# Sliding windows by DMA alone: a twelfth staged batch, and packets of 16 and 32 KB on two rings

## The chip, the cores and the metric

The kernel runs on one core of a Trainium2 chip. The metric is the time of one execution on the device in microseconds; the number given is the median of three runs. One more execution is recorded by the hardware profiler, and the views quoted here come from that execution.

## The reference

The input `x` has 32 batches of 4096 rows of 256 float32 values. Windows of 64 rows are taken at every 32nd row, 127 per batch, and each window is copied to its place in the output:

```python
n_windows = (length - window_size) // stride + 1        # 127
result = np.zeros((batch, n_windows, window_size, dim), dtype=np.float32)
for i in range(n_windows):
    start = i * stride
    result[:, i] = x[:, start:start + window_size].copy()
```

There is no arithmetic. A block is 32 rows, 32 KB; a batch is 128 blocks, 4 MB. A window is two neighbouring blocks, 64 KB, so nearly every block is written twice: once as the second half of a window and once as the first half of the next. The output of a batch is 127 windows, about 8 MB.

## The kernel before

The kernel consists of DMAs and waits only; no compute engine works on data. A batch reaches the output in one of two ways.

*Copied batches* (21 of 32) go from DRAM to DRAM. `_Kernel.copy` (L91) issues three DMAs on SP's queue for each: windows 0 to 63 (`WHOLE = 64`), windows 64 to 111, and the last 15. Source rows of 64 KB start 32 KB apart and so overlap; output rows of 64 KB lie behind each other. `start` (L59) takes `parts`, which limits the size of a piece to 64 KB divided by `parts`: the first 64 windows go in pieces of 64 KB, the rest in pieces of 32 KB.

*Staged batches* (11 of 32, the odd numbers 1 to 21 in `STAGED`) go through SBUF, on ACT's queue. `load` (L73) reads a batch into one of five tiles (`BUFS`) of 128 partitions of one 32 KB block each; `store` (L81) writes the tile out twice, as the first halves of the windows and as the second halves. All pieces are 32 KB. Each store covers 128 windows where a batch has 127: the surplus half window falls into the neighbouring batch's output, the first half of the next batch's window 0 or the second half of the previous batch's last window. That is why the staged batches are every other one, and why the neighbours of a staged batch have to be written after its stores.

ACT's loop issues load n+1, waits for load n, and issues the two stores of batch n. From the sixth load on, a load waits for the stores that used its tile five batches earlier.

SP issues the copies in the order that `_order` (L99) gives. The `EARLY` batches (18, 20, 22) come first: they are copied before their staged neighbours are stored, ACT waits for them (`all_of`, L63) before the first store beside them, and their damaged half windows are written again at the end, by small DMAs of one block in 16 pieces of 2 KB (`half`, L44). Then come batches without a staged neighbour. A batch with staged neighbours (a "tied" one) is put in at a position worked out from the last staged neighbour's place `behind`, `ceil((behind + 2) * n / len(STAGED))` with n = 21 copied batches, and before it SP waits for the stores of its neighbours (`after_store`, L69).

At the end SP waits for the stores beside the early batches and for the early copies, issues the small DMAs for the damaged halves, and then waits for everything.

Of the kernel before, what the change touches and what calls it, by code (L numbers as in the profile page):

```python
# [1 line left out]

# [4 lines left out]


STAGED = tuple(range(1, 22, 2))
BUFS = 5  # L10

WHOLE = 64

EARLY = (18, 20, 22)


class _Geometry:


    def __init__(self, x, out, W, S):  # L20
        self.B, self.L, self.D = x.shape
        self.x, self.out = x, out
        self.n_win = (self.L - W) // S + 1
        self.n_blk = self.L // S
        self.blk = S * self.D
        self.win = W * self.D
        assert W == 2 * S and self.n_blk == self.n_win + 1 == 128

    def src(self, b, block, dims):

        at = (b * self.n_blk + block) * self.blk
        return bass.AP(self.x.tensor, self.x.offset + at, dims)

    def dst(self, b, half, dims):

        at = b * self.n_win * self.win + half * self.blk
        return bass.AP(self.out.tensor, self.out.offset + at, dims)

    def rows(self, b, w0, n):

        s, d = [[self.blk, n], [1, self.win]], [[self.win, n], [1, self.win]]
        return self.dst(b, 2 * w0, d), self.src(b, w0, s)

    def half(self, b, half, block):  # L44

        dims = [[self.blk // 16, 16], [1, self.blk // 16]]
        return self.dst(b, half, dims), self.src(b, block, dims)


class _Kernel:  # L50
    def __init__(self, nc, g, tiles):
        self.nc, self.g, self.tiles = nc, g, tiles
        self.loaded = [nc.alloc_semaphore(f"loaded{i}") for i in range(len(tiles))]
        self.stored = [nc.alloc_semaphore(f"stored{i}") for i in range(len(tiles))]
        self.copied = nc.alloc_semaphore("copied")
        self.early = nc.alloc_semaphore("early")
        self.count = {}

    def start(self, engine, out, in_, sem, parts=1):  # L59
        engine.dma_start(out=out, in_=in_, max_dma_last_dim=65536 // parts).then_inc(sem, 16)  # L60
        self.count[id(sem)] = self.count.get(id(sem), 0) + 16

    def all_of(self, engine, sem):  # L63
        engine.wait_ge(sem, self.count[id(sem)])

    def slot(self, n):
        return divmod(n, len(self.tiles))

    def after_store(self, engine, n):  # L69
        turn, i = self.slot(n)  # L70
        engine.wait_ge(self.stored[i], 32 * (turn + 1))

    def load(self, n):  # L73

        g, (_, i) = self.g, self.slot(n)
        if n >= len(self.tiles):
            self.after_store(self.nc.scalar, n - len(self.tiles))
        src = g.src(STAGED[n], 0, [[g.blk, g.n_blk], [1, g.blk]])
        self.start(self.nc.scalar, self.tiles[i][:, :], src, self.loaded[i])

    def store(self, n):  # L81

        g, (turn, i) = self.g, self.slot(n)
        self.nc.scalar.wait_ge(self.loaded[i], 16 * (turn + 1))
        for half in (0, -1):
            dst = g.dst(STAGED[n], half, [[g.win, g.n_blk], [1, g.blk]])
            self.start(self.nc.scalar, dst, self.tiles[i][:, :], self.stored[i])

    def copy(self, b, sem):  # L91

        n, nc = self.g.n_win, self.nc
        self.start(nc.sync, *self.g.rows(b, 0, WHOLE), sem)
        self.start(nc.sync, *self.g.rows(b, WHOLE, n // 16 * 16 - WHOLE), sem, 2)
        self.start(nc.sync, *self.g.rows(b, n // 16 * 16, n % 16), sem, 2)


def _order(B):  # L99


    near = {b for s in STAGED for b in (s - 1, s + 1)}
    order = list(EARLY) + [b for b in range(B) if b not in near and b not in STAGED]
    tied = sorted(near - set(EARLY))
    n = len(order) + len(tied)
    for b in tied:
        behind = max(STAGED.index(s) for s in (b - 1, b + 1) if s in STAGED)
        order.insert(-(-(behind + 2) * n // len(STAGED)), b)
    return order


@with_exitstack
def kernel(
    ctx: ExitStack,
    tc: tile.TileContext,
    x: bass.AP,
    window_size: bass.AP,
    stride: bass.AP,
    out: bass.AP,
):  # L120
    nc = tc.nc
    W, S = int(window_size), int(stride)
    g = _Geometry(x, out, W, S)
    assert 0 not in STAGED and g.B - 1 not in STAGED
    pool = ctx.enter_context(tc.tile_pool(name="blocks", bufs=1))
    tiles = [pool.tile([g.n_blk, g.blk], x.dtype, name=f"xb{i}") for i in range(BUFS)]

    with tc.tile_critical():
        k = _Kernel(nc, g, tiles)
        for b in _order(g.B):  # L130
            if b not in EARLY:
                for s in (b - 1, b + 1):
                    if s in STAGED:
                        k.after_store(nc.sync, STAGED.index(s))
            k.copy(b, k.early if b in EARLY else k.copied)
        k.load(0)
        waited = False
        for n, s in enumerate(STAGED):
            if n + 1 < len(STAGED):
                k.load(n + 1)  # L140
            if not waited and (s - 1 in EARLY or s + 1 in EARLY):
                k.all_of(nc.scalar, k.early)
                waited = True
            k.store(n)


        for n, s in enumerate(STAGED):
            if s - 1 in EARLY or s + 1 in EARLY:
                k.after_store(nc.sync, n)
        k.all_of(nc.sync, k.early)  # L150
        for b in EARLY:
            if b - 1 in STAGED:
                k.start(nc.sync, *g.half(b, 0, 0), k.copied)
            if b + 1 in STAGED:
                k.start(nc.sync, *g.half(b, 2 * g.n_win - 1, g.n_blk - 1), k.copied)
        for n in range(len(STAGED)):
            k.after_store(nc.sync, n)
        k.all_of(nc.sync, k.copied)
        for sem in [*k.loaded, *k.stored, k.copied, k.early]:
            nc.sync.sem_clear(sem)  # L160


# [1 line left out]
_INS = ['x', 'window_size', 'stride']  # L164
_OUTS = [((32, 127, 64, 256), 'float32')]

_NUMBERS = {'window_size': 64, 'stride': 32}


# [26 lines left out]
```

## Time and profile before

| what | value |
|---|---|
| median of 3 runs | 770.55 us (769.2 to 771.77) |
| the profiled execution's own time | 772.19 us |
| span in that profile | 770.4 us |
| DMA packets, bytes | 9890, 313.37 MB |
| HBM read, written | 221.09 MB, 267.22 MB |
| copies issued by SP (64, 48 and 15 windows) | 21 of each |
| loads and stores issued by ACT, 4096 KB each | 11 and 22 |
| small DMAs for damaged halves, 32 KB each | 5 |

The span is what the profiler recorded between the first and the last instruction; the device time is a little longer. Queue q1 is SP's ring and q10 is ACT's. Both rings are served by the same sixteen DMA engines. GB/s in the profile counts each byte that a DMA moves once: a copied byte counts once although it is read from and written to HBM. Because no compute engine works, the parts of the page on engines and the chain of work that ended last are nearly empty (four constants set by POOL), and the reading goes by the DMA lines, the waits of SP's queue and the trace's record of every DMA packet (its queue, size, start and duration).

### The profile page before, as it was taken

How to read it: one execution, taken by the hardware profiler on the slowest of the kernel's cores; microseconds unless marked ns; L12 is line 12 of the kernel's file. 1: busy time of each engine (PE TensorE's matmuls, PEld its weight loads, DVE VectorE, ACT ScalarE, POOL GpSimd, SP SyncE). 2: the span in 40 equal slices, each digit the busy share in tenths (PEclk: the TensorE clock that was granted, in tenths of full speed). 3: DMA queues.
4: the chain of work that ended last, by engine and by line, in shares of the span. 5: the costliest groups of instructions: out<-in, count | busy, mean ns of one | idle time of the engine just before them, and what ended most of it. 6: DMA issues, size and time to landing. Idle time of an engine off the chain costs nothing. (4 is left out here: it accounts for less than half of the span.)

```text
span 770.4 us, 179 instructions
## 1 busy us (share of the span) xinstructions
POOL 0.2 (0%) x4
## 2 busy tenths in 40 slices
POOL 0000000000000000000000000000000000000000
DMA  9999999999999999999999999999999999999994
GB/s 381 396 412 436 393 413 419 447 371 434 400 424 395 441 403 424 403 444 386 430 420 422 405 419 419 403 412 419 417 415 427 417 415 412 444 415 432 391 338 178
DMA packets 9890, 313.37 MB, mean 407 GB/s; under 512 B 1595, under 2 KB 1595, under 8 KB 1675
## 3 DMA queue, kind: packets, MB, share of 16 engines
q1 hardware_dynamic: 5137, 174.95, 55.3%
q10 hardware_dynamic: 4752, 138.41, 43.2%
q14 instruction: 1, 0.01, 0.0%
HBM read 221.09 MB, written 267.22 MB: 634 GB/s over the span
## 5 line engine op out<-in xcount | busy, mean ns | idle before, releaser
L177 POOL MEMSET const-bfloat16-1.0<- 128x1 bf16 x1 | 0.1, 101 | 0.0
L177 POOL MEMSET const-uint8-127<- 128x1 uint8 x1 | 0.1, 101 | 0.0
L177 POOL MEMSET const-float32-0.0<- 128x1 f32 x1 | 0.1, 98 | 0.2 <-issue 0.2
L177 POOL MEMSET const-float32-1.0<- 128x1 f32 x1 | 0.1, 98 | 0.0
## 6 DMA issues: line engine op xcount, KB each, us to landing
out_dram<-xb ACTq DMA_DIRECT2D x22, 4096.0 KB, 94.1
out_dram<-in_x_dram SPq DMA_DIRECT2D x21, 3072.0 KB, 118.5
xb<-in_x_dram ACTq DMA_DIRECT2D x11, 4096.0 KB, 129.6
out_dram<-in_x_dram SPq DMA_DIRECT2D x21, 960.0 KB, 124.8
out_dram<-in_x_dram SPq DMA_DIRECT2D x21, 111.2
out_dram<-in_x_dram SPq DMA_DIRECT2D x5, 32.0 KB, 23.1
```

The source lines that it names most:

```text
L177: nc = _bacc.Bacc("TRN2", target_bir_lowering=False, num_devices=1)
```

## The change

`STAGED` grows by batch 23, so that 12 batches are staged and 20 are copied. Loads and stores go in pieces of 16 KB (`2 * BLOCK_PARTS` is 4). A copied batch is issued as 80 windows in pieces of 16 KB, 32 windows in pieces of 32 KB and 15 windows in pieces of 16 KB (`COPY_PARTS`). `EARLY` gets batch 24, the other neighbour of batch 23. In `_order` a tied batch's position takes `behind + 2.5` instead of `behind + 2`. At the end, the small DMAs for the damaged halves are issued store by store, each as soon as its own store has landed, where before all the stores concerned were awaited first; there are seven of them instead of five.

```diff
-STAGED = tuple(range(1, 22, 2))
+STAGED = tuple(range(1, 24, 2))
 BUFS = 5
-WHOLE = 64
-EARLY = (18, 20, 22)
+EARLY = (18, 20, 22, 24)
+BLOCK_PARTS = 2
+COPY_PARTS = ((80, 4), (32, 2), (15, 4))
...
     def load(self, n):
...
-        self.start(self.nc.scalar, self.tiles[i][:, :], src, self.loaded[i])
+        self.start(self.nc.scalar, self.tiles[i][:, :], src, self.loaded[i], 2 * BLOCK_PARTS)
...
     def store(self, n):
...
-            self.start(self.nc.scalar, dst, self.tiles[i][:, :], self.stored[i])
+            self.start(self.nc.scalar, dst, self.tiles[i][:, :], self.stored[i], 2 * BLOCK_PARTS)
...
     def copy(self, b, sem):
-        n, nc = self.g.n_win, self.nc
-        self.start(nc.sync, *self.g.rows(b, 0, WHOLE), sem)
-        self.start(nc.sync, *self.g.rows(b, WHOLE, n // 16 * 16 - WHOLE), sem, 2)
-        self.start(nc.sync, *self.g.rows(b, n // 16 * 16, n % 16), sem, 2)
+        w = 0
+        for rows, parts in COPY_PARTS:
+            self.start(self.nc.sync, *self.g.rows(b, w, rows), sem, parts)
+            w += rows
+        assert w == self.g.n_win
...
-        order.insert(-(-(behind + 2) * n // len(STAGED)), b)
+        order.insert(-(-(2 * behind + 5) * n // (2 * len(STAGED))), b)
...
+        k.all_of(nc.sync, k.early)
         for n, s in enumerate(STAGED):
             if s - 1 in EARLY or s + 1 in EARLY:
                 k.after_store(nc.sync, n)
-        k.all_of(nc.sync, k.early)
-        for b in EARLY:
-            if b - 1 in STAGED:
-                k.start(nc.sync, *g.half(b, 0, 0), k.copied)
-            if b + 1 in STAGED:
-                k.start(nc.sync, *g.half(b, 2 * g.n_win - 1, g.n_blk - 1), k.copied)
+            if s - 1 in EARLY:
+                k.start(nc.sync, *g.half(s - 1, 2 * g.n_win - 1, g.n_blk - 1), k.copied)
+            if s + 1 in EARLY:
+                k.start(nc.sync, *g.half(s + 1, 0, 0), k.copied)
```

More of the change, by code (lines that the diff above doesn't have):

```diff
@@ L137 @@
         waited = False
+        last = len(STAGED) - 1
         for n, s in enumerate(STAGED):
-            if n + 1 < len(STAGED):
+            if n < last:
                 k.load(n + 1)
```

## The prediction

> **What bounds the kernel now.** I read the page's slices and queues first. In the slices, the reader should see that the DMA engines are busy to the last slice but one, while the rate wanders from 371 to 447 GB/s and falls to 178 only at the end.
>
> ```profile
> DMA  9999999999999999999999999999999999999994
> GB/s 381 396 412 436 393 413 419 447 371 434 400 424 395 441 403 424 403 444 386 430 420 422 405 419 419 403 412 419 417 415 427 417 415 412 444 415 432 391 338 178
> DMA packets 9890, 313.37 MB, mean 407 GB/s; under 512 B 1595, under 2 KB 1595, under 8 KB 1675
> ...
> q1 hardware_dynamic: 5137, 174.95, 55.3%
> q10 hardware_dynamic: 4752, 138.41, 43.2%
> ...
> HBM read 221.09 MB, written 267.22 MB: 634 GB/s over the span
> ```
>
> Queue q1 is SP's ring (the copies), q10 is ACT's (staged loads and stores). Together they fill 98.5% of sixteen engines' time, so no engine can be kept busier and no wait hides much. Less time means fewer bytes, or packets that run faster. The waits agree: SP sits 601.5 us behind stores, yet its packets go on at an even rate in every stretch of the records, so its ring is never empty meanwhile.
>
> ```profile
> SPq L71 <- DMA out_dram<-xb: 601.5, 9, 97.0
> SPq L60 <- DMA out_dram<-xb: 85.8, 1, 85.8
> SPq L64 <- DMA out_dram<-in_x_dram: 26.3, 1, 26.3
> ```
>
> The windows show the end. The last store lands at about 738 us (SP issues its last small copies at 738.6), and from there only copies run, much more slowly.
>
> ```profile
> 380.00:420.00 40.00, 0.00 (x0) 1.00 1.01 425
> 420.00:460.00 40.00, 0.00 (x0) 1.00 1.00 406
> ...
> 700.00:737.00 37.00, 0.00 (x0) 1.00 0.97 406
> 737.00:768.00 31.00, 0.00 (x0) 1.00 0.72 257
> ```
>
> Then I tallied the trace's packet records by size. A 32 KB packet takes 1213 ns at best, and 75% of them are within 2 ns of that; the mean is 1254 (copies) and 1260 (staged). A 64 KB packet takes 2418 at best, reached by only 35%; the mean is 2584. A completion record takes 9 ns, and a packet starts 4 ns before its predecessor ends. So an undisturbed packet costs 37.66 ns per KB plus about 4 ns, and everything above that I call stall.
>
> An engine has this work. Copies of 64, 48 and 15 rows give it 4 packets of 64 KB, 6 of 32 KB and 2 of 32 KB per batch. The 15 rows run on 15 engines (q1's 1067 completion records are 42 x 16 + 21 x 15 + 5 x 16), so the sixteenth has less and does not decide. Copy batch: 4 x 2.414 + 8 x 1.209 = 19.33 us; 21 of them are 405.9. Staged batch: one load and two stores of 8 packets, 24 x 1.209 = 29.02; 11 of them are 319.2. With completions the undisturbed work is **725.6 us**. The records' own time on such an engine is 759.2, so stall is **33.6**; the span's other **11.2** are ends (first packet about 2.8 us in, last landing to span end 1.8, the rest engines that finish unevenly).
>
> Where the stall sits: I cut the trace into 5 us stretches and set stall against the copies' share of the bytes. A copied byte is read from and written to HBM, a staged one only read or only written, so HBM traffic is 1 + share per DMA byte. Stretches with a share above 0.62 (41 of 144, 205 us) lose 7.5%, or 15.4 us; the others lose 2.5%, or 12.7 us; those at 0.47 to 0.52 lose 1.6%, with a median of 0.4%. With copies alone at the end 18 to 23% is lost (about 5 us), and at the start 0.7. High shares come when 64 KB copy packets meet 32 KB staged ones: the rings alternate packet by packet, completions included (4627 records on q1 against 4676 on q10 between about 10 and 730 us), so a packet twice as long takes twice the share, 0.667.
>
> **The change, part by part.** *One more batch staged.* It adds 29.02 and removes 19.33 us of work per engine: +9.7 us, all on the path, since the engines have no idle time to put it in. It saves 4.1 MB of HBM reads.
>
> *Smaller packets.* A 16 KB packet has no row in this trace. Between zero and the 4 ns of the larger sizes I take 4, giving 606.5 ns undisturbed. Copies: 24 x 0.6065 + 4 x 1.209 = 19.39, times 20 = 387.8. Staged: 48 x 0.6065 = 29.11, times 12 = 349.3. With completions this makes **737.6**, 12.0 above before: 9.7 from the batch, 2.3 from packet ends.
>
> *What meets what.* 24 of a copy batch's 28 packets now equal the staged ones, a share of 0.5. Only the 32 rows in 32 KB packets make 0.667: 4 turns x 1.82 = 7.3 us of a batch's 36.5 us, 20%, against 4 x 3.62 = 14.5 of 37.4, 39%, before. High shares held 28% of the steady time (engines drift out of step); scaled by 20/39 that is 14.6%. Steady stall is then 0.146 x 7.5% + 0.854 x 1.6% = 2.5% of some 748 us, 18.4. I take 1.6% because that row has the mix the new kernel has; the ends are 0.4% (its median, were the rest spilt over from neighbouring stretches) and 2.5% (all stretches below 0.62), worth 10.8 and 24.2 us.
>
> *The end.* Per engine, q1 now has 20 x (28 + 3) = 620 records and q10 12 x (48 + 3) = 612; before, 315 and 297. SP's ring starts about 4.4 us later, some 7 small packets. So copies run alone for 15 packets of 0.6 us, 9 us, instead of 31, and lose 1.6 instead of about 5. Start: 0.7 as before. Total stall **20.7**. Uneven finishes come from uneven stalls; with about 40% less stall I take 2.5 off the ends, **8.7** (bounds: 11.2, and 4.6 for the latencies alone).
>
> *Waits and order.* `_order` puts a tied copy half a step later and `EARLY` has one more, so five copies instead of four are issued before SP's first wait. SP's stores come back well ahead: it now issues at 95.8 us the copies that start near 133, a lead of 38; in the new order a store ends every 63 us (750 us over twelve), the first near 84, and a copy batch starts every 37.5 us, so that the batch behind store 0 (the sixth, at 187) has a lead of about 100, behind store 1 (the seventh, at 225) 78, and the later ones 75 to 100. A later issue would cost nothing until the ring ran dry. ACT's wait for `early` stands at store 8, some 530 us in, with the four early copies done by about 150. The last halves go from five to seven (32 more packets of 2 KB at about 84 ns over 16 engines: 0.2 us). The last two wait for the last store, behind which 9 us of copies still run and cover two issues of 0.6 us. If the staged ring ended last they would cost about 3 us (1.2 plus 1.9 from issue to first packet, as at the start).
>
> Sum: 737.6 + 20.7 + 8.7 = **767.0 us** of span against 770.4, 3.4 less. The profiled execution took 772.19, and the runs' median is 770.55; 3.4 off the median gives **767.0**, rounded.
>
> Rules that bear on this. The 7.5% above a share of 0.62 and the 323 to 345 GB/s of copies alone (twice that through HBM, up to 690) say that mixing decides. The Trainium skill (HBM Reference, Specifications) gives about 716 GB/s for one HBM domain; an estimate from that page is that a share of 0.667 could still run at about 430 GB/s, so unmixing would bring almost nothing and the sum would be 737.6 + 33.6 + 11.2 = 782. I go by the row. The Trainium skill (DMA: Bandwidth & Descriptors, Latency and other measured facts) also reports that row pitches of large powers of two slow copies; an engine's 64-row share steps 256 KB in the output before and 320 KB with 80 rows, and were that the cause instead, the sum would lose another 6 us (0.146 x the 5.9% between 7.5 and 1.6, of 748). No run here separates the two yet.
>
> **The rivals.**
> *Deeper gain, 0.18.* Even mixing nearly ends the stall: 0.4% in even stretches saves 7.6 more, **759.4**. For it: many 5 us stretches at a share near 0.5 show none at all. Against: the mean is 1.6%.
> *A draw, 0.20.* Stall in even stretches is 2.0% instead of 1.6% (2.6 us more, span 769.6), or the ends stay at 11.2 (769.5), or both (772.1): the gain from mixing then pays for the twelfth batch and no more.
> *Slower, 0.25.* Stall follows bytes, whatever meets what: today's 32 KB records stand 3.4 and 3.8% above their best, and 3.6% of 737.6 is 26.6, with ends of 11.2 **775.4**. It decides once stall passes 24.1 us, or 3.3% of the work (21.6 if the ends don't shrink). Within it, 0.04 for stall per packet: 44 ns on each of 1136 packets is 50 us, **799**. For it: 32 KB records beside 64 KB ones are hardly slower than elsewhere. Against: 64 KB packets reach their best half as often as 32 KB ones, and stall peaks once per copied batch.
> The forecast itself, 0.37, spans 763 to 769 by its own bounds.
>
> **How the numbers follow.** A difference of 0.3% (2.3 us) is about what a measurement can tell here. The forecast and the deeper gain make faster 0.55; the draw makes same 0.20; slower is 0.25. The range leaves out the deepest gain and the per-packet case: 757 to 778, taking in 759.4 and 775.4 with two microseconds about them.
>
> **What would show it.** Right: 16 KB records at 610 ns for most, mean at most 625; q10 ending about 10 us before q1; slices steadier, near 420 to 430 GB/s with no dips below 400; DMA bytes 317.4 MB. Wrong: a 16 KB mean above 633 (stall by bytes), a best above 615 (a price per packet), q10 ending last, or dips that remain with even packets.

## The result, and the profile after

The changed kernel takes 767.25 us (median of 6 runs, 766.43 to 768.4) where the kernel before takes 770.95 (6 runs beside it). The ratio is 0.9949, with a 95% interval of 0.9936 to 0.9962: faster by half a per cent. The profiled execution took 768.4 us, its span is 766.6.

The page's slices, queues and HBM line after the change, to be laid beside those of before:

```profile
DMA  8999999999999999999999999999999999999996
GB/s 371 425 410 421 405 428 431 408 411 427 423 415 421 431 415 425 432 408 416 427 420 417 431 420 420 423 428 410 414 427 419 422 428 418 417 428 421 420 406 237
DMA packets 19837, 317.70 MB, mean 414 GB/s; under 512 B 1628, under 2 KB 1628, under 8 KB 1740
...
q1 hardware_dynamic: 10044, 166.70, 51.9%
q10 hardware_dynamic: 9792, 151.00, 47.3%
...
HBM read 217.02 MB, written 267.35 MB: 632 GB/s over the span
```

Three things are to be seen. The engines move 4.3 MB more and are about as full as before (99.2% against 98.5%), so most of the gain is in how fast packets run. The dips are gone: from the second slice to the last but one the rate lies between 405 and 432, where before it swung from 371 to 447 up to the last two slices. And the two rings hold nearly equal numbers of records (10044 and 9792).

The windows of the end: the staged ring is done at 754 us, and copies run alone for 10 us instead of 31.

```profile
700.00:737.00 37.00, 0.00 (x0) 1.00 0.98 416
737.00:754.00 17.00, 0.00 (x0) 1.00 0.96 401
754.00:764.00 10.00, 0.00 (x0) 1.00 0.55 198
```

The waits of SP's queue (who waited for what; us in total, times, longest) show a change that the prediction did not have:

```profile
SPq L62 <- DMA out_dram<-xb: 61.2, 2, 40.2
SPq L73 <- DMA out_dram<-xb: 19.2, 3, 9.4
SPq L66 <- DMA out_dram<-in_x_dram: 7.7, 1, 7.7
```

SP waited 714 us for stores and copies before and 88 us now. It spends the difference inside its DMA instructions. The durations of these issues (line L62; min/median/max in ns) have become very long:

```profile
L62 SPq DMA_DIRECT2D out_dram<-in_x_dram x67: 510/8114/29578, 0.9 to 756.2; - x67
L62 ACTq DMA_DIRECT2D out_dram<-xb x24: 378/442/625, 20.9 to 672.9; - x24
L62 ACTq DMA_DIRECT2D xb<-in_x_dram x12: 418/13034/19682, 0.9 to 550.1; - x12
```

Before, the medians were 597 ns on SP and 500 ns for ACT's loads; all of SP's DMA instructions together took 50 us before and take 672 now. A load now has twice the packets per engine, and a copied batch 28 where it had 12. I read this as a queue ahead of the engines that fills up, so that the issuing instruction stands until there is room.

**The sum, measured.** By the same tally of packet records, for one of the fifteen full engines:

| us | before | predicted | after |
|---|---|---|---|
| undisturbed work | 726.0 | 737.6 | 738.8 |
| stall | 33.4 | 20.7 | 19.4 |
| ends | 11.0 | 8.7 | 8.5 |
| span | 770.4 | 767.0 | 766.6 |

The tally here takes the undisturbed 16 KB record at its measured 611 ns, and means without the early rounding; that is why before differs by 0.2 to 0.4 from the prediction's figures. Of the 14.0 us less stall, some 10 are steady stall (28.1 and 18.1 us between 5 and 725 us) and most of the rest is the stretch of copies alone at the end.

### The profile page after: what moved, and what is told of

Read it like the earlier page. It is cut to its first block, busy times and chain, and to the rows that moved or that the text cites. A ratio compares the mean times of both kernels' runs of the same rounds, so it can differ in the third digit from the quotient of the medians.

```text
span 766.6 us, 180 instructions
## 1 busy us (share of the span) xinstructions
POOL 0.2 (0%) x4
## 3 DMA queue, kind: packets, MB, share of 16 engines
q1 hardware_dynamic: 10044, 166.70, 51.9%
q10 hardware_dynamic: 9792, 151.00, 47.3%
```

## The experiments

Two theories stood against each other. **Mixing**: stall goes by the copies' share of the bytes that run at a time, since a copied byte passes HBM twice. **Size**: small packets stall less, whatever runs beside them. Two more were to be excluded: that the twelfth batch's saved HBM reads, or the windows' steps in memory, make the gain. All results in one table; "share" and "steady stall" are the means over the 5 us stretches between about 5 and 725 us, "swing" the standard deviation of the share, ratio that to the kernel before, run beside it, with its 95% interval. Work and ends are tallied as above; what the span has beyond the two is stall. Each tally is of the one profiled execution, which lies up to about 1.5 us from its kernel's median, so one or two microseconds between rows say little. How many stretches lie above some share also depends on where the stretches begin (28 to 44 of 144 lie above 0.62 in before); what they lose moves less (7.0 to 7.9%).

| kernel | median us | ratio | span | work | ends | share | swing | steady stall |
|---|---|---|---|---|---|---|---|---|
| before | 770.95 | 1 | 770.4 | 726.0 | 11.0 | 0.548 | 0.098 | 3.9% |
| changed | 767.25 | 0.9949 (0.9936 to 0.9962) | 766.6 | 738.8 | 8.5 | 0.521 | 0.057 | 2.5% |
| uneven | 793.2 | 1.0276 (1.0250 to 1.0302) | 792.5 | 737.6 | 12.3 | 0.563 | 0.200 | 5.75% |
| double | 770.27 | 0.9987 (0.9974 to 0.9999) | 768.0 | 736.0 | 8.6 | 0.513 | 0.074 | 2.6% |
| half | 771.69 | 0.9995 (0.9983 to 1.0008) | 770.1 | 742.4 | 10.7 | 0.525 | 0.054 | 2.2% |
| double_level | 769.32 | 0.9970 (0.9958 to 0.9983) | 768.7 | 735.9 | 10.6 | 0.527 | 0.072 | 3.0% |
| b12_large | 777.88 | 1.0083 (1.0062 to 1.0104) | 775.0 | 735.8 | 10.2 | 0.546 | 0.095 | 3.9% |
| b11_small | 766.28 | 0.9934 (0.9914 to 0.9954) | 765.3 | 728.5 | 8.9 | 0.555 | 0.068 | 3.6% |
| before_tail | 775.42 | 1.0045 (1.0029 to 1.0062) | 773.7 | 725.9 | 10.5 | 0.564 | 0.109 | 5.0% |
| pow2 | 769.35 | 0.9971 (0.9958 to 0.9984) | 767.4 | 738.9 | 8.9 | 0.513 | 0.059 | 2.2% |
| b13 | 772.2 | 1.0004 (0.9990 to 1.0019) | 770.5 | 749.1 | 7.0 | 0.490 | 0.040 | 2.0% |
| b12_even | 767.77 | 0.9953 (0.9939 to 0.9966) | 766.2 | 738.7 | 10.5 | 0.528 | 0.053 | 2.3% |
| b11_even | 768.45 | 0.9963 (0.9951 to 0.9976) | 768.2 | 728.4 | 12.0 | 0.565 | 0.043 | 3.8% |
| b10_even | 767.22 | 0.9946 (0.9927 to 0.9965) | 765.3 | 718.3 | 10.9 | 0.593 | 0.036 | 4.9% |

All edits are to the changed kernel.

### Mixing or size: uneven, double, half

```diff
 # uneven
-COPY_PARTS = ((80, 4), (32, 2), (15, 4))
+COPY_PARTS = ((80, 2), (32, 2), (15, 2))
```

> The changed kernel with all copy packets at 32 KB (380 records per engine on the copies' ring against 612 on the staged one), so that 32 KB copy packets meet 16 KB staged ones and copies hold a share of 0.667 wherever both rings have work; staged packets go alone for the rest. Undisturbed work 737.0 us per engine, 1.2 below the changed kernel's. Mixing theory (stall goes by the copies' share): 7.5 to 8% of the 617 us of shared work, 46 to 49 us of stall, and with ends of 8 a span of 785 to 795. Size theory (small packets stall less, whatever meets what): stall of 20 to 24 us, span 765 to 769.

Span 792.5 with 42.7 us of stall: the mixing theory's 785 to 795, and far from the size theory's 769. Bytes and HBM reads are those of the changed kernel and work is 1.2 us less; only the sizes that meet are others. The page's slices lie below the changed kernel's nearly everywhere, mostly between 385 and 420:

```profile
GB/s 366 396 392 411 393 394 402 403 401 414 422 411 385 417 418 405 393 429 403 423 429 409 389 409 413 408 400 420 395 427 413 404 397 419 400 405 402 402 426 189
...
HBM read 217.02 MB, written 267.35 MB: 611 GB/s over the span
```

Fifteen of its 5 us stretches hold almost only staged packets (share below 0.2), and these lose 0.5%; those above 0.62 lose 7.1%, close to the 7.5% that the prediction read off the trace of before.

In these kernels a high share always comes from copy packets twice as large as the staged ones that they meet, so unequal sizes as such were not tried apart from the share. What speaks for the share is where one ring runs alone and nothing is mixed: staged packets alone lose 0.5%, copies alone some 17 to 18% (the ends of before, double and pow2).

```diff
 # double
-BLOCK_PARTS = 2
-COPY_PARTS = ((80, 4), (32, 2), (15, 4))
+BLOCK_PARTS = 1
+COPY_PARTS = ((80, 2), (32, 1), (15, 2))
 # half
+BLOCK_PARTS = 4
+COPY_PARTS = ((80, 8), (32, 4), (15, 8))
```

> The changed kernel with every packet twice as large (staged 32 KB, copies 32 and 64 KB), so that shares stay the same. Undisturbed work 735.4 us. Records per engine 340 on the copies' ring against 324, so copies run alone for some 26 us instead of 10. Mixing theory: steady stall of 2.4 to 2.5% as in the changed kernel, 18 us, 4 for the end alone, 0.7 at the start, ends 9: span 767. Size theory: stall of 32 KB packets as in the kernel before, 3.6%, 26.5 us, and ends of 11: span 773 or more.

> The changed kernel with every packet half as large (staged 8 KB, copies 8 and 16 KB), shares unchanged. Some 1050 more packets per engine at 4 ns: undisturbed work 742.7 us. Mixing theory: stall as in the changed kernel, 20 us, ends 8: span 770 to 772. Size theory: stall falls again, to 13 us or less, span 764 or below.

Spans of 768.0 and 770.1 are near what mixing expected (767, and 770 to 772) and far from size (773 or more, and 764 or below). Steady stall is 2.6%, 2.5% and 2.2% from doubled to halved packets, so size has a small part of its own at most, under half a point over a factor of four. The halved kernel is less clean than its span: with 8 KB records at the 309 ns that 94% of them take, its whole stall is 17.0 us, halfway between mixing's 20 and size's 13, and ends of 10.7 where 8 was expected make up for it. Its packet ends cost 3.6 us of work. The doubled kernel's median is 3.0 us above the changed one's and its span only 1.4, because the profiled execution of the changed kernel was the slowest of its six (1.15 us above the median) and that of the doubled one lay 0.5 below.

### Which part of the change gains: b12_large, b11_small

```diff
 # b12_large: twelve staged batches with the packets of before
+BLOCK_PARTS = 1
+COPY_PARTS = ((64, 1), (48, 2), (15, 2))
 # b11_small: eleven staged batches with small packets
+STAGED = tuple(range(1, 22, 2))
+EARLY = (18, 20, 22)
+COPY_PARTS = ((64, 4), (48, 2), (15, 2))
```

> Twelve staged batches with the packet sizes of before (staged 32 KB; 64 windows at 64 KB, 48 and 15 at 32 KB): 300 records per engine on the copies' ring against 324. Undisturbed work 735.3 us. Mixing theory: high shares as before the change, steady stall 3.9%, 28.7 us, no stretch of copies alone, 0.7 at the start, ends 9, and up to 3 for the last small copies that nothing covers: span 774 to 777, slower than before. If the saved HBM reads were what helped, the span would be 763 to 767 like that of the changed kernel.

> Eleven staged batches as before the change, but staged packets of 16 KB and copies of 64 windows at 16 KB, 48 at 32 KB, 15 at 32 KB: 567 records per engine against 561, so that the rings end together. Undisturbed work 728.1 us. Mixing theory: 40% of a batch's time has a share of 0.667, as before the change (39%), so steady stall stays near 3.9%, 28 us, 2 for start and end, ends 9.5: span 768. Size theory: stall 2.5%, 18 us, 2 and 8.4: span 757, better than both kernels.

The twelfth batch alone makes the kernel slower by 0.8%: +9.8 us of work, and steady stall stays at 3.9%. The saved HBM reads bought nothing in steady stall; the 4.4 us less stall in all (29.0 against 33.4) are about what copies alone had lost at the end of before. This kernel also has the new order of copies and the new order of the last small DMAs, so those do not lower steady stall either. Small packets with eleven batches are faster by 0.66%. Their stall is 27.9 us, 2 less than mixing expected and 8 more than size did; with ends of 8.9 the span is 3 us lower than mixing said. Against before, its steady stall is only some 2 us lower (3.6% against 3.9%); at the end it saves some 3 us of stall and 2.1 of ends, and it pays 2.5 us of work for the packets. Beside the changed kernel's 0.9949 (0.9936 to 0.9962) its 0.9934 (0.9914 to 0.9954) is not told apart. So the gain needs the packets and not the twelfth batch. From eleven batches to twelve stall falls (27.9 to 19.4) for about as much work (728.5 to 738.8). The batch alone does not do that: with it, the copied batches' windows in 32 KB packets go from 63 to 32, since fewer large ones are needed to keep the rings level.

### The level end alone: before_tail, double_level

```diff
 # before_tail: eleven batches, packets of before, rings level
+STAGED = tuple(range(1, 22, 2))
+EARLY = (18, 20, 22)
+BLOCK_PARTS = 1
+COPY_PARTS = ((80, 1), (32, 2), (15, 2))
 # double_level
+BLOCK_PARTS = 1
+COPY_PARTS = ((80, 2), (32, 1), (15, 1))
```

> Eleven staged batches and packets of 64 and 32 KB as before, but 80 windows at 64 KB instead of 64: 294 records per engine against 297, so that both rings end together. Undisturbed work 725.6 us as before. Mixing theory: a share of 0.667 for 50% of a batch's time instead of 39%, steady stall 4.3% or 31.5 us instead of 28; the stretch of copies alone goes (1 instead of 5 us) and ends shrink by 0 to 2.5: span 768 to 770.5. If the even end alone were the change's gain: 762 to 764.

> The doubled kernel (staged 32 KB, copies of 80 windows at 32 KB and 32 at 64 KB) with its last 15 windows in 64 KB packets too, which takes one record per batch off the copies' ring: 320 per engine against 324, where the doubled kernel had 340 and ran copies alone for 27 us. Undisturbed work 735.9 us. Mixing theory: the 3.8 us of stall at the end go; the 15 windows meet staged packets at a share of 0.667 for one more turn in sixteen, which adds about 0.3%, 2 us, to a steady 18.8; ends 8.6 or up to 2 more if the staged ring ends last: span 765 to 767.5, about the changed kernel's 766.6. If level ends were worth more than that (the rings' ends set the span): 762 or less.

In both, the rings now end within 3 us of each other, and neither kernel gains on the one that it is levelled from (before, and double) beyond noise. The first is slower than before by 0.45%: 16 more windows at 64 KB raise the stretches above 0.62 from 41 to 58 and their loss from 7.5% to 9.3%. That is 3 us beyond what mixing expected and the opposite of what a level end should bring. In the second the 3.8 us at the end went and came back as 2.5 us of steady stall and 2 us of ends; its median is 0.95 us below that of double. Both kernels bought the level end with more windows at a high share; a level end without that was not tried alone.

The ends column suggests a price of small copies that nothing covers: where the staged ring ended last or level with the other, ends are 10.2 to 12.3 us (uneven, half, double_level, b12_large, before_tail, the three even kernels); where copies ended last, 7.0 to 8.9, with the kernel before (11.0) as the one exception.

### Steps of a power of two: pow2

```diff
+COPY_PARTS = ((64, 4), (16, 4), (32, 2), (15, 4))
```

> The changed kernel with its 80 windows of 16 KB packets issued as 64 and 16: an engine's share of the 64 then steps 256 KB in the output, a power of two, as before the change, instead of 320 KB. One more completion record per batch (640 per engine against 612), so copies run alone for some 21 us instead of 10. Mixing theory: about 2.3 us more at the end, span 768 to 769. Address theory (steps of a power of two cause the stall of the 64-window part): some 6 us of steady stall come back as well, span 773 to 775.

Span 767.4, with 3.8 us of stall at an end of 25 us instead of 0.4, and 2.2% of steady stall, not more than the changed kernel's 2.5%. The slowing at row pitches of large powers of two that the Trainium skill reports (DMA: Bandwidth & Descriptors, Latency and other measured facts), with figures from a pitch of 512 KiB up, is not seen in these copies. Steps of 256 KB cost nothing here.

### More staging, and even shares: b13, b12_even, b11_even, b10_even

```diff
 # b13
+STAGED = tuple(range(1, 26, 2))
+EARLY = (18, 20, 22, 24, 26)
+COPY_PARTS = ((80, 4), (32, 4), (15, 4))
 # b12_even
+COPY_PARTS = ((16, 4), (16, 2)) * 3 + ((16, 2), (15, 2))
 # b11_even
+STAGED = tuple(range(1, 22, 2))
+EARLY = (18, 20, 22)
+COPY_PARTS = ((16, 2),) * 7 + ((15, 4),)
 # b10_even
+STAGED = tuple(range(1, 20, 2))
+EARLY = (16, 18, 20)
+COPY_PARTS = ((32, 2),) + ((16, 2),) * 5 + ((15, 2),)
```

> Thirteen staged batches, every packet 16 KB (665 records per engine against 663), so that the share is 0.5 all the way. Undisturbed work 748.3 us, 10.1 above the changed kernel's. Mixing theory: stall at a share near 0.5 is 1.6 to 1.9%, 12 to 14 us, 2 for start and end, ends 8: span 770 to 773, slower than the changed kernel. If even mixing ended the stall (0.4%): 761 to 762.

> Twelve staged batches as in the changed kernel, a copied batch issued as eight DMAs of 16 windows (the last of 15), three of them in 16 KB packets and five in 32 KB packets, alternating; 600 records per engine against 612. Undisturbed work 738. Even share near 0.52 to 0.55 in every 8 us. Mixing theory: stall 1.6 to 2.3%, 12 to 17 us, 1 for the start, ends 8: span 759 to 764, a few us below the changed kernel. Size theory: more 32 KB packets than the changed kernel has, so stall of 20 to 22 us: 767 to 769.

> Eleven staged batches with staged packets of 16 KB as in b11_small, but a copied batch issued as seven DMAs of 16 windows in 32 KB packets and one of 15 windows in 16 KB packets. Per engine a DMA of 16 windows is two 32 KB packets and a completion record, three turns against three staged packets, so the copies' share is near 64/112 = 0.57 in every 4 us instead of swinging between 0.5 and 0.667. 546 records per engine against 561. Undisturbed work 728. Mixing theory: at an even share of 0.57 stall is some 2.3 to 3%, 17 to 22 us, 1 for the start, ends 8 to 9, perhaps 3 for small copies at the end that nothing covers: span 755 to 760, faster than both kernels. Size theory: copies are mostly 32 KB packets, which stall 3.5% or more, so 25 to 28 us: span 763 to 766.

> The same with ten staged batches and 22 copied: a copied batch is one DMA of 32 windows, five of 16 and one of 15, all in 32 KB packets; 506 records per engine against 510. Undisturbed work 717.5 us. Even share 0.59 to 0.6 throughout. Mixing theory: a share of 0.6 all the time stands where stall rises (stretches of 0.57 to 0.62 lost 3 to 6%), 23 to 40 us, 1 for the start, ends 9: span 751 to 768, the middle at 759. Size theory: 3.5% or 25 us, 1 and 9: 753.

With thirteen batches the share is lowest and so is stall, and the span is 770.5 as expected: 10.3 us more work than the changed kernel against 5.0 less stall (14.4) and 1.5 less at the ends. Two of the three even kernels missed mixing's range, and the third, b10_even, stayed inside a wide one (765.3 in 751 to 768), 6 us above its middle and 12 above size's 753. b12_even lost 2 us less to stall than the changed kernel and gave 2 back at the ends. b11_even is 8 us above its expected 760: its share was held near 0.565 with hardly a swing, and it still lost 3.8%. Its 27.9 us of stall are what size expected (25 to 28) and not what mixing did (17 to 22), though its span missed size's 763 to 766 too. b11_small, with the same batches, nearly the same share and a wider swing, lost as much. So at a share of 0.56 to 0.6 it no longer helps to even things out; stretches between 0.57 and 0.62 lost 4.0% there and 4.5% in b10_even.

Stall follows the level of the share here: in before, the changed kernel and b13 alike, stretches at 0.47 to 0.52 lose some 1.6%, and those at 0.52 to 0.57 some 3 to 5%.

Three kernels have the same mean share by chance: b11_even, before_tail and uneven (0.565, 0.564, 0.563), with swings of 0.043, 0.109 and 0.200. They lose 3.8, 5.0 and 5.75%. That fits a stall set by the mean share and its swing, but the three differ in packet sizes as well. With ten, eleven and twelve batches the medians are 767.2, 766.3 and 767.3, a flat bottom on which each batch more, with packets chosen to fit it, costs about 10 us of work and saves 8 to 11 us of stall.

## Why the prediction was right

*The work* was sized right: 12.8 us more, against 12.0. The undisturbed 16 KB record takes 611 ns (predicted 610.5), and the batch's +9.7 is all there in b12_large (+9.8 of work, and no gap to hide it in).

*Stall by share* held as a mechanism: uneven brings it back at will (42.7 us), and equal ratios nearly keep the steady stall through a doubling and a halving of sizes. The term for steady stall came out at 18.1 us where 18.4 was forecast, but two parts of it were off and cancelled. I put 14.6% of the time above a share of 0.62, at 7.5%; it was 11 stretches of 144, 7.6%, at 4.0%. I took 1.6% for the rest, from the row of shares 0.47 to 0.52; it was 2.4%. So 1.1% became 0.3%, and 1.4% became 2.2%. The row itself held: stretches at 0.47 to 0.52 lost some 1.6% again. What the forecast left out is that about 40 of the 144 stretches stood between 0.52 and 0.62, where 3.4 to 4.8% is lost. That the two errors are of one size is luck; the draw's condition, 2.0% outside the high shares, was met and passed.

*The end* was right in kind: copies alone for 10 us (9 forecast), 0.4 us lost there (1.6), and ends of 8.5 (8.7). Why the ends shrank is not shown: b10_even has more stall than before (36.1 us) and ends of 10.9, b11_small 27.9 and 8.9, so they do not simply follow stall. One latency was misread: in the trace of before, the first packet starts 1.9 us into the span and not 2.8, 1.0 us behind its issue and not 1.9. That makes the price of small copies without cover 2.2 us instead of about 3, and the ends of the experiments suggest some 2.

*Waits and order* was wrong, at no cost. I had SP issue five copies at once and meet its first wait early, with a lead of 75 to 100 us. It cannot: its first seven DMAs, 83 records per engine, each took under 1 us to issue, and the eighth stood for 15. Room in the ring, as I read these times, and no longer the stores sets when SP issues, and as long as the ring is full that does not matter.

*The rivals.* Stall by bytes (775.4) falls to uneven; stall per packet to half, which has twice the packets of the changed kernel and 17.0 us of stall against 19.4. The deeper gain (759.4) falls to b13: at an even 0.49 the stall is 2.0%, not 0.4. Of the signs named, 89% of the 16 KB records take 611 ns and their mean is 626, a nanosecond above the limit set for it.

*The rule weighed.* The Trainium skill (HBM Reference, Specifications) gives about 716 GB/s per domain; by an estimate from that, a share of 0.667 should have run almost freely, and the sum was 782. It did not: uneven lost 7.1% above 0.62. Some of its 5 us stretches carried some 735 GB/s through HBM without any stall, but no kernel here carried more than 714 over 15 us or 700 over 20 us. So the figure is not contradicted as a ceiling. Why stall begins well below it is not shown by a rate alone.

## What to carry to other kernels

Where two rings feed the same DMA engines, their records alternate, and packet sizes decide whose bytes run together: choose them so that copies within HBM do not hold a high share for long beside transfers through SBUF, and count completion records as turns. Evening the ratio out further brought nothing here (b12_even against the changed kernel). Work that lowers one resource's load by loading another (a staged batch here) has a flat best; find the level where an added unit of work buys just as much stall, and look for the gain in how the two are mixed. A tally of packet times against the best time of each size tells undisturbed work, which can be forecast closely, from stall, which has to be tried.

## What was not expected of the hardware

The stall that is left over is densest while a staged batch is loaded. I assigned each packet record to a load or a store by the order of the completion records on ACT's ring. In the changed kernel packets lose 4.1% while ACT's ring loads and 1.7% while it stores, at the same copies' share of 0.52; with thirteen batches it is 4.4% against 0.6%. The windows of the kernel with thirteen batches show it on the page's own scale: first four load stretches, then four store stretches (the last column is GB/s).

```profile
140.00:161.00 21.00, 0.00 (x0) 1.00 1.01 412
200.00:220.00 20.00, 0.00 (x0) 1.00 1.01 415
259.00:279.00 20.00, 0.00 (x0) 1.00 1.00 411
318.00:338.00 20.00, 0.00 (x0) 1.00 1.01 413
```

```profile
161.00:200.00 39.00, 0.00 (x0) 1.00 1.00 427
220.00:259.00 39.00, 0.00 (x0) 1.00 1.01 429
279.00:318.00 39.00, 0.00 (x0) 1.00 1.01 429
338.00:377.00 39.00, 0.00 (x0) 1.00 1.01 429
```

Two bytes are read for each one written in the first, one for two in the second. The same order shows in kernels with 64 KB packets: about 5% against a little over 3% both before the change and in b12_large. Only in uneven the two are nearly alike (about 5 and 6%). So the change took little from the load stretches (about 5% to 4) and halved the stall of the store stretches (over 3% to 1.7), and the mixing account explains the second better than the first. Whether it is the reads themselves, or where the loads and the copies read, was not tried.

SP's ring also seems to have limited room: SP stood in its eighth DMA with 83 records per engine issued ahead of it, while in the kernel before, twelve DMAs with 60 records went out within 9 us. It is not a fixed number of records, as SP first stood with 73 ahead in uneven and with 100 in half; what sets it was not tried.
